# adaLN steps in groups of three from three buffers, none until the RWKV scan is over; pairs in the FFN

## The chip, the cores and the metric

The kernel runs on one core of one Trainium2 chip. The metric is the device time of the execution in microseconds (us); the time before is the median of three runs. TensorE (PE in the profile) multiplies matrices, VectorE (DVE), ScalarE (ACT) and GpSimd (POOL) do the elementwise work, and SyncE (SP) issues nearly all DMA transfers, in the order of its queue.

## The reference, cut to what matters

One layer of a diffusion backbone, in float32, with D = 2048, 256 latent tokens and 256 context tokens. The parts that the change touches are the adaLN vectors and what uses them:

```python
mod_x = (jax.nn.silu(c) @ w_mod[l] + b_mod[l])[:, None, :]          # w_mod: 2048 x 12288
sh1x, sc1x, gt1x, sh2x, sc2x, gt2x = jnp.split(mod_x, 6, axis=-1)
ux = modulate(rms_norm(x, norm_g[l, 0]), sh1x, sc1x)
mc, mx = token_mixers(uc, ux, p, not last)                            # conv, mLSTM, GDN, RWKV, gates, merge, w_out
x = x + gt1x * rms_norm(mx, norm_g[l, 1])
fx = conv_ffn(modulate(rms_norm(x, norm_g[l, 2]), sh2x, sc2x), ffn_up[l], ffn_dw[l], ffn_down[l], True)
x = x + gt2x * rms_norm(fx, norm_g[l, 3])
```

`token_mixers` projects the modulated input with w_in into the columns of four branches and four sets of gates, runs three chunked scans in two directions (RWKV, gated DeltaNet or GDN, mLSTM) and a convolution module, multiplies each branch by its w_br, sums them under sigmoid gates and multiplies by w_out.

## The kernel before, in words

**Column sets.** A weight matrix is read in loads of 256 x 512 floats (512 KB, `raw`). ScalarE rounds each to `hi` (fp32r) and VectorE subtracts to get `lo` (lines 198 and 200); the activations are kept split the same way (`uh`, `ul`). A set of 512 columns takes eight loads ("kg"). `mode_b` makes columns by tokens (`psB`), `mode_a` tokens by columns (`psA`); each kg costs three products per 128 rows, per block or token tile, all issued in `mm` (line 79). After each kg both call `feed()`.

**adaLN steps.** `wmod_steps` makes 512 columns of the adaLN vector in eight steps: each loads 512 KB of w_mod (`wraw`, line 260) and issues four products of 32 columns (`psw`; the profile has eight records a step). The eighth is followed by a copy of the sums (`wrows`), products that spread them (`psf`) and an addition of the bias into `mod2`, or, for the two gain vectors `G[0]` and `G[1]`, an addition and a product by the norm's gain over 128 partitions, with two 256 KB rows loaded into `wbg`. `psw` and `psf` take turns in the one PSUM bank of the pool `wap` before the FFN, and in the two banks of `auxf` in it. The opening stage makes the first eight blocks itself, from a pool of seven buffers. `mod_feed` is the generator of the rest: eight blocks of `mod2` (64 steps), four of G[0] (32), four of G[1] (32). `feed()` adds `rate` to `fed` and takes steps until `modn` has caught up, up to `modmax`.

**Order.** `build` calls, one after another: the opening stage, RWKV columns and scan, GDN columns, mLSTM columns, conv columns, two gate column sets, the RWKV output, the GDN scan, the conv module, the mLSTM scan, the sixteen column sets of `gates` (16 x 8 kgs), four `merge`s (16 column sets of two kgs each, so 32 kgs), `out_proj` (w_out), and `ffn`. The program is ordered by a scheduler that follows these priorities and a timing model, so scans are threaded through the column sets that come after them in the source: the scans' small products run as they become ready, and column products fill the time between. The order on each engine and in the SP queue is then fixed. Gates write their sigmoids to HBM (`dg`); a merge reads them back (`sig`) and accumulates in `mg`.

**The pace before.** `rate` is 0 until the mLSTM columns, 0.55 from there, 0 again after the gates; in the FFN it is 0.25, after a first block of eight steps at its start (`feed(96 + 8)`). Step loads go into the pool `wmr` with one buffer; in the FFN they take a tile of the ring of `raw` (five).

**SBUF.** Pools are placed when the scheduler reaches them, where there is room; a tile in a reused place waits until the tiles that were there have been read. `g1p` holds G[0] and is opened in `gd_scan`; `mqT` and `mkT` lie in the mLSTM scan's pool `mrp`; `mgw` (for `sig`), `mgp` (for `mg`) and `hlp` (a second ring of hi and lo for the last set of `out_proj`) are opened after the gates, in this order. `stage` hands out tiles of 512 floats from `fs` under the tags f0 to f3.

Of the kernel before, what the change touches and what calls it, by code (L numbers as in the profile page):

```python
# [11 lines left out]
F32 = mybir.dt.float32  # L12
# [8 lines left out]
P = 128  # L21
D = 2048
# [19 lines left out]
class Kern:  # L42
# [205 lines left out]
    def wmod_steps(self, cb, dst, raws=None, gain=None):  # L248


        nc, A = self.nc, self.A
        if raws is not None and cb in (0, 4):
            ps = self.mmp.tile([P, 512], F32, tag="mm", name="psw")
        else:
            ps = (self.evp if self.wap is not None else self.aux)("psw")
        w = A["w_mod"][0]
        for j in range(8):
            wr = raws or self.wmr
            raw = self.raw() if wr is None else wr.tile([P, 2, 512], F32, tag="wraw", name="wraw")
            nc.sync.dma_start(out=raw, in_=w[256 * j : 256 * j + 256, 512 * cb : 512 * cb + 512].rearrange("(k p) c -> p k c", p=P))  # L260
            for k in range(2):
                for h in range(2):
                    r = slice(64 * h + 32 * k, 64 * h + 32 * k + 32)
                    self.mm(ps[r, 0:256], self.cst[:, 2 * j + k, :], raw[:, k, 256 * h : 256 * h + 256], start=(j == 0), stop=(j == 7))
            if j < 7:
                yield
        rows = self.stage("f3", 256, "wrows")
        nc.scalar.activation(rows, ps[:, 0:256], AF.Copy)
        if gain is not None:

            bg = self.stage("f2", 512, "wbg"), self.stage("f2", 512, "wbg")
            for t, row in zip(bg, (A["b_mod"][0], gain)):
                c0 = 512 * cb if row is not gain else 512 * (cb % 4)
                nc.sync.dma_start(out=t, in_=row[c0 : c0 + 512].unsqueeze(0).to_broadcast([P, 512]))
            ps = (self.evp if self.wap is not None else self.aux)("psf")
            for h in range(2):
                self.mm(ps[:, 256 * h : 256 * h + 256], self.selb[:, h], rows)
            nc.vector.tensor_tensor(dst, ps, bg[0], ALU.add)
            nc.gpsimd.tensor_tensor(dst, dst, bg[1], ALU.mult)
            yield  # L280
            return
        ps = (self.evp if self.wap is not None and raws is None else self.aux)("psf")
        for i in range(2):
            self.mm(ps[:, 4 * i : 4 * i + 4], rows[:, P * i : P * i + P], self.sel4.rearrange("p h c -> p (h c)"))
        n = dst.shape[2]
        bm = self.PC["b_mod"][:, 4 * cb : 4 * cb + 4].unsqueeze(2).to_broadcast([P, 4, n])
        for h in range(2):
            nc.vector.tensor_tensor(dst[:, 2 * h : 2 * h + 2], ps[:, 0:8].rearrange("p (i h c) -> p h i c", h=2, c=2)[:, h, :, 0:n],
                                    bm[:, 2 * h : 2 * h + 2], ALU.add)
        yield  # L290
# [14 lines left out]
    def feed(self, upto=0):  # L305

        self.fed += self.rate
        while self.modn < max(upto, min(self.fed, self.modmax)):
            self.modn += 1
            next(self.modgen)  # L310

# [183 lines left out]

    def stage(self, tag, shape, name):

        t = self.fs.tile([P, 512], F32, tag=tag, name=name)
        return t if shape == 512 else t[:, 0:shape]

    def rw_k_steps(self):
# [517 lines left out]
    def gd_scan(self):  # L1019
# [2 lines left out]
        ges = ExitStack()  # L1022
        up = self.pool("gup", stack=ges, side="right")
        wp = self.pool("gwp", bufs=2, stack=ges, side="right")
        self.G[0] = self.pool("g1p", stack=self.ues).tile([P, D], F32, name="G1")
        tp = self.pool("gtp", stack=ges, side="right")
        lg, beta = self.lg, self.beta
        b4 = lambda ap, r=P: ap.unsqueeze(2).to_broadcast([r, 4, P])
# [22 lines left out]
        for nm, src in (("negc", negc), ("egc", egc), ("erem", erem), ("beta", beta)):  # L1051
            t = m4[nm] = gp.tile([P, 2, 4, 4], F32, name="gm" + nm)
# [18 lines left out]
        for seg in range(2):  # L1071
# [5 lines left out]
            for jj in range(2):  # L1077
# [13 lines left out]
                for h in range(4):  # L1091
                    for c in range(2):
                        r = slice(64 * c, 64 * c + 64)
                        t = slice(P * jj + 64 * c, P * jj + 64 * c + 64)
# [10 lines left out]
            for i in range(4):  # L1105
# [6 lines left out]
                for d in range(2):  # L1112
                    t = slice(256 * seg + 64 * ch[d], 256 * seg + 64 * ch[d] + 64)
# [69 lines left out]
    def ml_scan(self):  # L1183
        nc = self.nc
        self.mlx = ExitStack()
        mp = self.pool("mrp", stack=self.mlx)
        wa = self.pool("mwa", bufs=2, stack=self.mlx)
        wp = self.pool("mwb", bufs=2, stack=self.mlx)
        mqT, mkT = mp.tile([P, 4, 256], F32, name="mqT"), mp.tile([P, 4, 512], F32, name="mkT")
        mv = mp.tile([P, 4, 4, 132], F32, name="mv")  # L1190
        nc.gpsimd.memset(mv[:, :, :, 128:129], 1.0)
        nc.sync.dma_start(out=mqT, in_=self.dmq)
# [231 lines left out]
    def ffn(self):  # L1424
        nc, A, PC = self.nc, self.A, self.PC
        x = self.x1
        ues = ExitStack()
# [9 lines left out]
            nc.vector.tensor_scalar(diag[:, i], self.ident, rs[i], None, ALU.mult)  # L1437
        sc = fp.tile([P, KT], F32, name="sc2")
        nc.vector.scalar_tensor_tensor(sc, self.mod2[:, 16:32, 0], 1.0, PC["ng"][:, 32:48], ALU.add, ALU.mult)
        self.fs = self.pool("ffs", bufs=2)  # L1440
        self.wap, self.rate, self.modmax = None, 0.25, 128
        self.G[1] = fp.tile([P, D], F32, name="G2")
        self.feed(96 + 8)
# [101 lines left out]
    def build(self):  # L1545
        tc = self.tc
        pes = ExitStack()
        self.auxs = None
        self.aux_pool("auxp", aux=3)
        self.wap = self.pool("wap", bufs=1, space=PSUM, stack=pes)  # L1550
        self.mmp = self.pool("mmp", bufs=4, space=PSUM, stack=pes)
        self.constants()
        self.dp = self.pool("dp", space=bass.MemoryType.DRAM)
        ses = ExitStack()
        self.rawp = self.pool("rawp", bufs=4, stack=ses)
        self.hip = self.pool("hip", bufs=2, stack=ses)
        self.lop = self.pool("lop", bufs=2, stack=ses)
        ues = self.ues = ExitStack()
        self.up = self.pool("up", stack=ues)
        bp = self.bp = self.pool("bp", stack=ues)  # L1560
        self.wmr = self.pool("wmr", bufs=1, stack=ues)
        self.xes = ExitStack()
        self.x2 = self.pool("x2", stack=self.xes)
        fes = ExitStack()
        self.fs = self.pool("fs", bufs=2, stack=fes, side="right")
        res = ExitStack()
        rq = self.rqp = self.pool("rqp", stack=res, side="right")
        T = lambda nm, s: rq.tile(s, F32, name=nm)
        self.sxg = T("sxg", [P, 2, 256])
        self.bv = T("bv", [P, 4, 256])  # L1570
        self.res = res
        self.rwx = ExitStack()
        self.fed, self.rate, self.modn, self.modmax = 0.0, 0.0, 0, 96
        self.pool_lo = 0
        self.mod2, self.G = self.cp.tile([P, 32, 1], F32, name="mod2"), [None, None]
        self.modgen = self.mod_feed()
        self.phase0(self.rw_k_steps, self.rw_open)
        self.aux_pool("auxp2", aux=3)
        self.rw_columns()
        self.token_gates(bp)  # L1580
        self.rw_feat()
        self.aux_pool("auxr", u=2, s=1)
        self.rw_scan()
        self.gd_columns()
        self.rate = 0.55
        self.ml_columns()
        self.conv_columns()
        self.gz = self.gate_columns(C_GDZ, AF.Silu, "gz")
        self.mo = self.gate_columns(C_MLO, AF.Sigmoid, "mo")
        self.rw_out()  # L1590
        self.aux_pool("auxg", aux=3)
        res.close()
        ces = ExitStack()
        self.gop = self.pool("gop", stack=ces, side="right")
        self.cvp = self.pool("cvp", stack=ces, side="right")
        self.gd_scan()
        self.gd_out()
        self.conv_module()
        ces.close()
        self.ml_scan()  # L1600
        self.gates()
        self.feed(96)
        self.rate = 0.0
        fes.close()
        self.dbg("yh", self.uh[:, :, 0:256].bitcast(F32))
        self.dbg("yl", self.ul[:, :, 0:256].bitcast(F32))
        self.mgw = self.pool("mgw", bufs=3, stack=ues)
        self.mgp = self.pool("mgp", stack=ues)
        self.mg = self.mgp.tile([P, 2, D], F32, name="mg")
        self.hlp = self.pool("hlp", bufs=2, stack=ues)  # L1610
        self.resp = self.pool("resp", side="right")
        self.x1 = self.resp.tile([P, 2, D], F32, name="x1")
        self.ffdw = self.resp.tile([P, 396], F32, name="ffdw")
        self.nc.sync.dma_start(out=self.ffdw, in_=self.A["taps"])
        for i, n in enumerate((3, 0, 2, 1)):
            self.merge(i == 0, n)
        self.out_proj()
        self.wmr = None
        ues.close()
        ses.close()  # L1620
        pes.close()
        self.aux_pool("auxf", aux=2)
        self.es.callback(self.auxs.close)
        mes = ExitStack()
        self.mmp = self.pool("mmp2", bufs=6, space=PSUM, stack=mes)
        self.rawp = self.pool("rawp2", bufs=5)
        self.hip = self.pool("hip2", bufs=4)
        self.lop = self.pool("lop2", bufs=4)
        self.mmes = mes
        self.ffn()  # L1630

# [54 lines left out]
```

## Time and profile before

| | |
|---|---|
| median of 3 runs | 2329.59 us (2325.4 to 2334.24) |
| the profiled execution | 2329.05 us, span 2327.1 us, mean granted TensorE clock 0.977 |
| TensorE busy | 2215.9 us (95%) |
| VectorE, ScalarE, GpSimd busy | 1449.6, 989.5, 507.6 us |
| DMA | 471.97 MB, mean 203 GB/s |
| w_mod loads from wraw / raw | 160 / 32 of 512 KB |

The span is from the first to the last instruction; what lies around it is 1.9 us. TensorE's busy time counts products that overlap one another, and products that wait inside the array, so the cadence of starts in the timeline says more of its speed than the busy share. Rows of a timeline give start, duration, engine, line, operation, out<-in, tile and count, and in brackets the idle time before and what ended it. Rows of waits give the total, the number and the longest, in us.

### The profile page before, as it was taken

Reading aid. Unit: us, or ns where it says so; the run is one execution under the profiler, and the core shown is the slowest. Engines: PE = TensorE matmul, PEld = TensorE weight load, DVE = VectorE, ACT = ScalarE, POOL = GpSimd, SP = SyncE. Lnnn points to the kernel's source line nnn. Section 1 sums busy time; section 2 is a strip of 40 time slices with the busy share of each in tenths; the row PEclk is TensorE's granted clock in tenths of the full one; section 3 lists DMA queues with packets and bytes.
Section 4 is the critical chain, followed back from the end, with each engine's and each line's share of the span. In section 5 each row is a group of like instructions: output and inputs, shape, how many; then the busy total and the mean of one; then the engine's idle time right before and its main releaser. Section 6 shows DMA issues by size and latency. Waiting matters only on the chain.

```text
span 2327.1 us, 42867 instructions
## 1 busy us (share of the span) xinstructions
PE 2215.9 (95%) x16828; PEld 1812.0 (78%) x16828; DVE 1449.6 (62%) x3027; ACT 989.5 (43%) x1493; POOL 507.6 (22%) x865
## 2 busy tenths in 40 slices
PE   6979889999999989999999899989999999999998
PEld 3657667877888666777777678779999999998886
DVE  3357766734555678457565476577776677775554
ACT  4225644533554344334236434444443444444443
POOL 0012553533454599210010033010000000000000
PEclk8989999999999999999999999989999999999999
DMA  9934663555666776787777476567677666666663
GB/s 369 352 115 127 170 183 113 159 171 170 199 188 180 231 208 209 231 247 237 226 231 256 139 257 217 181 231 222 212 222 217 202 182 183 179 205 202 194 193 101
DMA packets 273867, 471.97 MB, mean 203 GB/s; under 512 B 41761, under 2 KB 80929, under 8 KB 272673
## 3 DMA queue, kind: packets, MB, share of 16 engines
q1 hardware_dynamic: 273378, 467.14, 64.8%
q8 instruction: 132, 2.16, 0.4%
q10 hardware_dynamic: 288, 2.10, 0.2%
q14 instruction: 69, 0.57, 0.1%
HBM read 440.33 MB, written 28.84 MB: 202 GB/s over the span
## 4 chain that ended last, share of the span: by engine, by line
PE 78%; DVE 8%; DMA 7%; POOL 4%; ACT 2%; issue 2%; SPq 0%; DVEq 0%; ACTq 0%; POOLq 0%
PE psB L79 37%; PE psA L79 18%; PE psD L79 10%; PE psw L79 4%; DMA wraw<-in_w_mod 3%; DVE lo L200 2%; POOL ctap L874 1%; DMA raw<-in_w_mix 1%; PE psG L79 1%; POOL cacc L875 1%; ACT hi L198 1%; PE psn L79 1%; DMA raw<-in_w_in 1%; PE psf L79 1%; DVE cacc L869 1%
## 5 line engine op out<-in xcount | busy, mean ns | idle before, releaser
L200 DVE TENSOR_TENSOR lo<-raw,hi 128x1024 fp32r<-128x1024 f32 (+2 forms) x485 | 599.2, 1236 | 458.7 <-ACT hi L198 450.0
L198 ACT ACTIVATE hi<-raw 128x1024 fp32r<-128x1024 f32 (+2 forms) x488 | 509.2, 1045 | 796.5 <-PE psB L79 348.6
L79 PE MATMUL psB<-u2h,hi 128*128 128x256 f32 x1408 | 399.5, 286 | 1.2 <-DVE u2h L1370 1.2
L79 PE MATMUL psB<-u2l,hi 128*128 128x256 f32 x1408 | 398.8, 284 | 0.5 <-DVE u2l L1371 0.5
L79 PE MATMUL psB<-u2h,lo 128*128 128x256 f32 x1408 | 399.0, 284 | 0.0
L79 PE MATMUL psA<-lo,uh 128*128 128x512 f32 x832 | 337.4, 406 | 18.4 <-DVE lo L200 18.0
L79 PE MATMUL psA<-hi,ul 128*128 128x512 f32 x832 | 332.7, 400 | 0.0
L79 PE MATMUL psA<-hi,uh 128*128 128x512 f32 x832 | 311.4, 405 | 3.2 <-DVE mg L1344 2.1
L79 PE MATMUL psB<-uh,hi 128*128 128x256 f32 (+1 forms) x832 | 281.0, 346 | 18.7 <-ACT hi L198 16.4
L79 PE MATMUL psB<-ul,hi 128*128 128x256 f32 (+2 forms) x832 | 278.5, 339 | 0.0
L79 PEld LDWEIGHTS psB<-u2h,hi 128*128 128x128 f32 x1408 | 269.6, 192 | 10.9 <-issue 9.5
L79 PEld LDWEIGHTS psB<-u2l,hi 128*128 128x128 f32 x1408 | 270.5, 192 | 0.7 <-DVE u2l L1371 0.7
L79 PE MATMUL psB<-uh,lo 128*128 128x256 f32 (+2 forms) x832 | 263.0, 339 | 8.1 <-DVE lo L200 8.1
L79 PEld LDWEIGHTS psB<-u2h,lo 128*128 128x128 f32 x1408 | 270.5, 192 | 0.1
L79 PEld LDWEIGHTS psA<-lo,uh 128*128 128x128 f32 x832 | 158.1, 190 | 68.5 <-DVE lo L200 27.5
L79 PEld LDWEIGHTS psB<-uh,hi 128*128 128x128 f32 x832 | 158.6, 191 | 51.2 <-ACT hi L198 18.5
L79 PEld LDWEIGHTS psA<-hi,uh 128*128 128x128 f32 x832 | 154.7, 190 | 53.2 <-issue 12.2
L79 PEld LDWEIGHTS psA<-hi,ul 128*128 128x128 f32 x832 | 158.3, 190 | 36.5 <-issue 2.6
L79 PEld LDWEIGHTS psB<-uh,lo 128*128 128x128 f32 (+1 forms) x832 | 152.8, 189 | 32.0 <-DVE lo L200 10.5
L79 PEld LDWEIGHTS psB<-ul,hi 128*128 128x128 f32 (+1 forms) x832 | 157.8, 190 | 23.1 <-issue 6.4
L1541 DVE TENSOR_TENSOR lo<-raw,hi 128x1024 fp32r<-128x1024 f32 x88 | 107.7, 1226 | 78.5 <-ACT hi L1540 78.5
L1461 DVE SCALAR_TENSOR_TENSOR facc<-fpad,ffdw,facc 128x256 f32<-128x256 f32 x352 | 152.8, 490 | 0.2
(573 smaller groups left out, 3028.8 us busy)
## 6 DMA issues: line engine op xcount, KB each, us to landing
raw<-in_w_in SPq DMA_DIRECT2D x208, 512.0 KB, 4.3
raw<-in_ffn_up SPq DMA_DIRECT2D x176, 512.0 KB, 3.8
wraw<-in_w_mod SPq DMA_DIRECT2D x160, 512.0 KB, 5.1
raw<-in_ffn_down SPq DMA_DIRECT2D x88, 512.0 KB, 4.5
raw<-in_w_br SPq DMA_DIRECT2D x32, 512.0 KB, 5.1
raw<-in_w_out SPq DMA_DIRECT2D x32, 512.0 KB, 4.4
raw<-in_w_mod SPq DMA_DIRECT2D x32, 512.0 KB, 3.8
raw<-in_w_in SPq DMA_DIRECT2D x48, 256.0 KB, 4.1
```

Source lines behind the costliest of these rows:

```text
L79: self.nc.tensor.matmul(out, lhsT, rhs, start=start, stop=stop)
L198: nc.scalar.activation(hi[s], raw[s], AF.Copy)
L200: (nc.gpsimd if self.pool_lo >= 0 else nc.vector).tensor_tensor(lo[s], raw[s], hi[s].bitcast(F32), ALU.subtract)
L869: nc.vector.scalar_tensor_tensor(a, cpad[:, i, t : t + 256], w(i, t), a, ALU.mult, ALU.add)
L874: nc.gpsimd.tensor_scalar(m, cpad[:, i, t : t + 256], w(i, t), None, ALU.mult)
L875: nc.gpsimd.tensor_tensor(a, a, m, ALU.add)
L1461: nc.vector.scalar_tensor_tensor(s3(acc), pad[:, dy : dy + 4, dx : dx + 64], tap(t, b), s3(acc), ALU.mult, ALU.add)
L1541: nc.vector.tensor_tensor(f(lo), f(raw), f(hi).bitcast(F32), ALU.subtract)
```

## The change

Steps are taken in groups: `feed` rounds what is due down to a multiple of `group`, 3 up to the merges and 2 in the FFN. `rate` stays 0 through all column sets and scans in the source and becomes 0.6 before `gates`; it goes on through the merges, after which `feed(96)` takes what is left. `wmr` has three buffers and is opened after the RWKV output; in the FFN a new `wmr2` has two, and steps no longer use `raw`. G[0] gets its place after the mLSTM scan. `mqT` and `mkT` get a pool of their own; `mg` is placed ahead of `mgw`; staging in the merges comes from a new pool `fsm`, which is closed with `mgw` before `hlp` is opened. In the FFN the staging tag f3 is 256 floats wide instead of 512. No product, load or elementwise operation is added or removed.

```diff
@@ wmod_steps
-            raw = self.raw() if wr is None else wr.tile([P, 2, 512], F32, tag="wraw", name="wraw")
+            raw = wr.tile([P, 2, 512], F32, tag="wraw", name="wraw")
@@ feed
         self.fed += self.rate
-        while self.modn < max(upto, min(self.fed, self.modmax)):
+        due = int(min(self.fed, self.modmax)) // self.group * self.group
+        while self.modn < max(upto, due):
@@ stage
-        t = self.fs.tile([P, 512], F32, tag=tag, name=name)
+        t = self.fs.tile([P, self.fw.get(tag, 512)], F32, tag=tag, name=name)
@@ gd_scan
-        self.G[0] = self.pool("g1p", stack=self.ues).tile([P, D], F32, name="G1")
@@ ml_scan
-        mqT, mkT = mp.tile([P, 4, 256], F32, name="mqT"), mp.tile([P, 4, 512], F32, name="mkT")
+        qk = self.pool("mqk", stack=self.mlx)
+        mqT, mkT = qk.tile([P, 4, 256], F32, name="mqT"), qk.tile([P, 4, 512], F32, name="mkT")
@@ ffn
-        self.fs = self.pool("ffs", bufs=2)
+        self.fs, self.fw = self.pool("ffs", bufs=2), {"f3": 256}
@@ build
-        self.wmr = self.pool("wmr", bufs=1, stack=ues)
...
-        self.fed, self.rate, self.modn, self.modmax = 0.0, 0.0, 0, 96
+        self.fed, self.rate, self.modn, self.modmax, self.group = 0.0, 0.0, 0, 96, 3
...
         self.gd_columns()
-        self.rate = 0.55
         self.ml_columns()
...
         ces = ExitStack()
+        self.wmr = self.pool("wmr", bufs=3, stack=ues)
...
         self.ml_scan()
+        self.G[0] = self.pool("g1p", stack=ues).tile([P, D], F32, name="G1")
+        self.rate = 0.6
         self.gates()
-        self.feed(96)
-        self.rate = 0.0
         fes.close()
-        self.mgw = self.pool("mgw", bufs=3, stack=ues)
         self.mgp = self.pool("mgp", stack=ues)
         self.mg = self.mgp.tile([P, 2, D], F32, name="mg")
-        self.hlp = self.pool("hlp", bufs=2, stack=ues)
+        mes = ExitStack()
+        self.fs = self.pool("fsm", bufs=2, stack=mes)
+        self.mgw = self.pool("mgw", bufs=3, stack=mes)
...
             self.merge(i == 0, n)
+        self.feed(96)
+        self.rate = 0.0
+        mes.close()
+        self.hlp = self.pool("hlp", bufs=2, stack=ues)
         self.out_proj()
-        self.wmr = None
...
+        self.wmr, self.group = self.pool("wmr2", bufs=2), 2
         self.mmes = mes
         self.ffn()
```

More of the change, by code (lines that the diff above doesn't have):

```diff
@@ L1564, in build @@
         fes = ExitStack()
-        self.fs = self.pool("fs", bufs=2, stack=fes, side="right")
+        self.fs, self.fw = self.pool("fs", bufs=2, stack=fes, side="right"), {}
         res = ExitStack()
```

## The prediction

> **What bounds the kernel now.** I read the page's engine table and chain first.
>
> ```profile
> span 2327.1 us, 42867 instructions
> ...
> PE 2215.9 (95%) x16828; PEld 1812.0 (78%) x16828; DVE 1449.6 (62%) x3027; ACT 989.5 (43%) x1493; POOL 507.6 (22%) x865
> ...
> PE 78%; DVE 8%; DMA 7%; POOL 4%; ACT 2%; issue 2%; SPq 0%; DVEq 0%; ACTq 0%; POOLq 0%
> PE psB L79 37%; PE psA L79 18%; PE psD L79 10%; PE psw L79 4%; DMA wraw<-in_w_mod 3%; DVE lo L200 2%; POOL ctap L874 1%; DMA raw<-in_w_mix 1%; PE psG L79 1%; POOL cacc L875 1%; ACT hi L198 1%; PE psn L79 1%; DMA raw<-in_w_in 1%; PE psf L79 1%; DVE cacc L869 1%
> ```
>
> TensorE is busy 95% of the span and carries 78% of the chain; the adaLN products (psw) are 4% of it and the wait for their weights 3%. That is an average, so next come the windows by stage (us; PE, PEld, DVE, ACT, POOL busy; clock; DMA share; GB/s): the column sets beside the RWKV scan (470 to 756), gates beside the conv module and the GDN scan (to 1280), the mLSTM scan's end (1280 to 1372; its worst part is 1303 to 1342), the merges (1342 to 1427), and a stretch of the start as the measure of a full DMA.
>
> ```profile
> 470.00:756.00 286.00, 286.00 (x3423) 231.19 (x3422) 141.44 (x542) 124.28 (x248) 119.28 (x349) 1.00 0.61 181
> 756.00:935.00 179.00, 162.78 (x1171) 115.59 (x1171) 138.83 (x281) 71.05 (x98) 144.09 (x145) 0.97 0.72 215
> 935.00:1280.00 345.00, 340.42 (x2671) 248.60 (x2666) 199.75 (x438) 138.80 (x184) 36.56 (x39) 1.00 0.78 239
> 1303.00:1342.00 39.00, 29.74 (x134) 23.12 (x132) 14.78 (x36) 12.56 (x29) 0.70 (x1) 0.82 0.36 123
> 1342.00:1427.00 85.00, 83.17 (x360) 66.33 (x361) 63.29 (x87) 32.01 (x38) 38.42 (x24) 0.98 0.79 269
> 58.20:116.40 58.20, 57.46 (x431) 37.24 (x423) 19.37 (x42) 13.88 (x21) 0.00 (x0) 1.00 1.00 352
> ```
>
> From 470 to 756 TensorE has no idle time at all, so an instruction taken from it there is time, unless a scan beside it sets the pace. From 935 to 1280 4.6 us are idle; at 1303 to 1342 nine are, at a clock of 0.82.
>
> **Price of a step, alone and in a row.** The timeline of TensorE around one step in the gates (eight records), then around five steps in a row in the opening stage:
>
> ```profile
> 1063.65 0.39 PE L79 MATMUL psA<-lo,uh 128*128 128x512 f32 x1
> 1063.88 0.39 PE L79 MATMUL psA<-hi,ul 128*128 128x512 f32 x1
> 1064.20 0.64 PE L79 MATMUL psw<-wraw,cst 128*32 128x256 f32 x8
> 1064.77 0.73 PE L79 MATMUL psA<-hi,uh 128*128 128x512 f32 x2
> 1065.34 0.39 PE L79 MATMUL psA<-lo,uh 128*128 128x512 f32 x1
> ...
> 63.87 2.37 PE L79 MATMUL psw<-wraw,cst 128*32 128x256 f32 x40
> 66.17 0.50 PE L79 MATMUL psB<-uh,hi 128*128 128x512 f32 x1
> ```
>
> Column products start 0.23 us apart. Around the lone step, three such starts (1063.88 to 1065.34) take 1.46 instead of 0.69: it costs 0.77 us. Five in a row take 2.30 from first start to the next psB; less the 0.57 from a lone step's start to its successor, four more cost 1.73, or 0.43 each. So a step directly behind another saves 0.34 us. Which steps are alone now is in the windows of the psw rows alone (PE and PEld busy, then ACT where the group has any):
>
> ```profile
> 470.00:756.00 286.00, 22.20 (x232) 5.35 (x232) 1.00 0.61 181
> 756.00:1300.00 544.00, 44.01 (x528) 10.78 (x528) 0.99 0.75 227
> 1570.00:2060.00 490.00, 14.06 (x176) 3.46 (x176) 1.10 (x3) 1.00 0.67 203
> ```
>
> 29 steps among the columns (0.77 us each), 66 from 756 on (0.67) and 22 in the FFN (0.64), nearly all lone; one more lies before 470.
>
> **The change part by part.** *Pace.* A feed comes after each of the kg loops. Before: 56 of them in the mLSTM, conv and gate columns at 0.55 give 31 steps, the rest come in the gates' 128. After: none in the columns; 0.6 over 128 feeds of gates and 32 of merges makes 96, in threes every fifth feed, 77 by the end of the gates and 19 in the merges. So the columns lose 31 steps (23.9 us at 0.77), the gates go from 65 to 77 steps, and the merges get 19, 10.3 us of TensorE at 0.77 + 2 x 0.43 = 1.63 per three.
>
> *Groups of three.* 32 groups, two steps of each behind another: 64 x 0.34 = 21.8 us less if all stay whole. A block has 8 steps, so 8 of the 12 blocks end inside a group; there the one PSUM bank (wap) must pass through ACT, psf and DVE before the next step, and other products go between. With some groups cut by a scan's products I keep 80%: **-17.4**. Ends: 0 and -21.8.
>
> *Three buffers.* Waits of TensorE from 935 to 1280, and of SP's queue from 756 to 1300:
>
> ```profile
> PE psw L79 <- DMA wraw<-in_w_mod: 4.0, 8, 1.2
> PE psA L79 <- DVE lo L200: 0.4, 1, 0.4
> ...
> SPq L194 <- DVE lo L200: 197.4, 78, 5.3
> SPq L260 <- PE psw L79: 53.5, 45, 3.1
> ```
>
> With one buffer a load is issued only behind the last step's products; SP then stands 53.5 us with the raw loads queued behind it, and TensorE waits 4.0. With three freed five feeds earlier both go: **-4.0** (ends 0 and -4.0); SP next waits for raw slots, as it does now for 197.4. Each moved step takes its load through the same SP queue, now three together, 1.57 MB, 4.5 us at 352 GB/s ahead of the next raw load; the four raw tiles cover 4 x 12 x 0.23 = 11 us. I cost it nothing; without that cover it is up to 4.5 us a group.
>
> *Places in SBUF* (wmr, mqk, G1, mgw behind mg, fsm, hlp): no instruction, but other waits on reused places. The timeline at the mLSTM scan's end:
>
> ```profile
> 1312.67 1.73 PE L79 MATMUL psn<-mv,mA 128*128 128x129 f32 x14
> ...
> 1336.81 3.35 PE L79 MATMUL psn<-mv,mA 128*128 128x129 f32 x14 [1.79 <-ACT mA L1259]
> ...
> 1342.25 0.50 PE L79 MATMUL psA<-hi,uh 128*128 128x512 f32 x1 [2.09 <-DVE mg L1344]
> ...
> 1341.51 2.48 DVE L1344 TENSOR_TENSOR mg<-sig,psA 128x512 f32<-128x512 f32 x4
> ```
>
> The merges fill their four PSUM banks and stop until mg is first written, after the scan's last psn. With other places that write can come up to 25 us earlier (1317, where the fill ended) or some 15 later, and the gates and columns run dry sooner, since 23.9 + 9 us of TensorE work leave ahead of this point. As TensorE never waits for a scan from 470 to 1280, I let the scans move up with it and take **+3** for a longer hole (ends -10 and +33). hlp's first use is three column sets of out_proj later (66 us); f3 at 256 and the dropped fallback to raw cost nothing.
>
> *Merges.* 85 us x 269 GB/s = 22.9 MB now; 19 loads of 512 KB and three pairs of 256 KB rows (wbg; sizes in the next fence) add 11.5 MB. 34.4 MB at 352 GB/s is 98 us, against 85 + 10.3 of TensorE: **+3** (ends 0 and +13). The Trainium skill ("DMA: Bandwidth & Descriptors", Measured) has 425 GB/s for a 16 MB transfer; by it the merges would take 81 us of DMA, this term would be 0 and the sum 3 us lower. No row quoted here is above 352.
>
> *FFN.* Pairs: of 22 lone steps 11 come to stand behind another, 11 x 0.34 = **-3.7** (ends 0, -3.7). But the first block of eight now has two buffers where it had five raw tiles:
>
> ```profile
> 1505.67 7.87 SPq L260 DMA_DIRECT2D raw<-in_w_mod  x5
> ...
> 1519.87 2.37 PE L79 MATMUL psw<-raw,cst 128*32 128x256 f32 x40
> ...
> 1534.48 2.67 PE L79 MATMUL psts<-ffdiag,x 128*128 128x128 f32 x10 [1.78 <-DVE ffdiag L1437]
> ...
> wraw<-in_w_mod SPq DMA_DIRECT2D x160, 512.0 KB, 5.1
> ...
> raw<-in_w_mod SPq DMA_DIRECT2D x32, 512.0 KB, 3.8
> ...
> wbg<-in_b_mod SPq DMA_DIRECT2D x8, 256.0 KB, 3.7
> ```
>
> Five loads are issued before out_proj ends and run as one row at 1519.87; the transposes wait for ffdiag until 1534.48. With two buffers it takes four rounds of 3.8 + 0.6 = 17.6 us, and if the place is out_proj's until 1519.5 the block ends at 1537 and holds one of two PSUM banks for 3 us of the transposes: **+2** (ends -1, +8). The five raw tiles then belong to ffn_up.
>
> **Sum**: -17.4 - 4.0 + 3 + 3 - 3.7 + 2 = -17.1. The profiled execution took 2329.05 us (span 2327.1 and 1.9 around it), the median of the three runs is 2329.59: 2329.05 - 17.1 = **2312**.
>
> **Rivals.** *The groups fall apart.* The loads of a group land one after another, and the order within TensorE's queue is made from ready times; if the steps are put singly into gaps, only the waits (-4.0) go and +8 of the costs stay, with nothing from the pairs: 2333 at worst, 2329 with half of those costs. For it: eight block ends inside groups. Against: all three loads can be issued five feeds ahead. *The scans set the pace (slower).* For: TensorE waits for ACT and DVE of the mLSTM scan from 1317 on. Against: no such wait before. Then nothing that leaves ahead of 1342 is gained, the hole grows, and the merges carry their 19 steps at the pace of the DMA: +13, FFN -3.7 + 2, and two more sets of psn at the low clock (3.35 against 1.73 us) +3.2: 2329 + 14.5 = 2343.5. It decides once more than about 20 of the 32.9 us come back as idle TensorE. The Trainium skill ("TensorE: Matmul & The Clock Gate", Part 1) halves the clock after about 3.4 us idle; the 0.82 above with waits of 2 us fits a partly cold stretch, and a longer hole would be colder. *The hole is filled.* Steps and merges run while the scan ends because mg comes early: -10 instead of +3, 2299. For: loads need only a free buffer. Against: G1's blocks need psf's bank.
>
> **Numbers.** Forecast 0.50 (own range 2301 to 2321), groups apart 0.22, scans 0.16, hole filled 0.12. A measurement of this kernel tells about 0.5% from no change, 2317.9 and 2341.2 here. Faster: the third and all below 2317.9 of the first, 0.12 + 0.40 = 0.52; slower: most of the scans' case, 0.13; same 0.35. Range 2298 to 2337: the filled hole to the groups apart, and the lower part of the scans' case.
>
> **What would show it.** psw rows of x24 (x16 in the FFN), none from 470 to 760, and TensorE's busy psw time per step near 0.5; no wait of psw for wraw; the gates' start earlier by some 20 us; DMA in the merges near 340 GB/s. Wrong would make it: psw rows of x8, idle of TensorE between the gates' end and mg's first write longer than 40 us, psA waiting for raw loads behind three wraw loads, or psts waiting past 1540 relative to out_proj's end.

## The result, and the profile after

The changed kernel takes 2354.11 us (median of 4 runs, 2351.78 to 2359.92) against 2327.49 for the kernel before: a ratio of 1.012, 95% interval 1.0105 to 1.0135. It is slower by 26.6 us, where 2312 was forecast. The profiled execution took 2354.46 us. From its page, the span, the engines and the group of adaLN products (busy, mean ns of one | idle before them and its releaser):

```profile
span 2352.5 us, 42883 instructions
...
PE 2219.5 (94%) x16828; PEld 1810.3 (77%) x16828; DVE 1450.7 (62%) x3027; ACT 980.9 (42%) x1488; POOL 505.9 (22%) x865
...
L79 PE MATMUL psw<-wraw,cst 128*32 128x256 f32 x1536 | 130.3, 407 | 47.6 <-DMA wraw<-in_w_mod 43.8
```

TensorE is busy 3.6 us longer than before, though groups were to save it time. psw waits 43.8 us for its own loads: 20.2 of them up to 470 us (22.2 before), 0.6 from 756 to 1300, and 23.0 at the start of the FFN, where steps waited 3.5 before. Three windows of the prediction, then the psw rows alone by stage:

```profile
470.00:756.00 286.00, 283.75 (x3275) 242.76 (x3274) 149.96 (x543) 137.03 (x262) 115.71 (x333) 1.00 0.50 145
...
1303.00:1342.00 39.00, 25.02 (x104) 17.72 (x105) 13.59 (x42) 5.63 (x19) 3.34 (x3) 0.63 0.30 91
1342.00:1427.00 85.00, 84.70 (x436) 61.64 (x434) 58.22 (x66) 29.95 (x35) 36.02 (x23) 1.00 0.92 332
```
```profile
470.00:756.00 286.00, 0.00 (x0) 0.00 (x0) 0.00 (x0) 1.00 0.50 145
756.00:1300.00 544.00, 57.77 (x640) 17.82 (x640) 3.36 (x9) 0.99 0.76 238
1300.00:1427.00 127.00, 11.91 (x128) 3.50 (x128) 1.11 (x3) 0.87 0.71 250
1570.00:2060.00 490.00, 13.46 (x192) 5.12 (x192) 1.15 (x3) 1.00 0.67 200
```

No step is left from 470 to 756, 80 stand from 756 to 1300 and 16 behind it. A step in the gates is busy for 57.77 / 80 = 0.72 us; before it was 0.67. At 1303 to 1342 TensorE is 14 us idle (9 before) at a clock of 0.63 (0.82 before). The timeline says how this stretch ends (TensorE, then VectorE, then the SP queue):

```profile
1324.65 3.35 PE L79 MATMUL psn<-mv,mA 128*128 128x129 f32 x14 [1.79 <-ACT mA L1260]
...
1333.19 2.79 PE L79 MATMUL psw<-wraw,cst 128*32 128x256 f32 x24 [3.52 <-DVE G L278]
1337.55 0.79 PE L79 MATMUL psA<-hi,uh 128*128 128x512 f32 x1 [1.56 <-DVE mg L1345]
...
1336.80 1.28 DVE L1345 TENSOR_TENSOR mg<-sig,psA 128x512 f32<-128x512 f32 x2 [3.66 <-DMA sig<-dg]
...
1328.15 0.34 SPq L274 DMA_DIRECT2D wbg<-in_b_mod  x1
...
1329.35 2.02 SPq L1339 DMA_DIRECT2D sig<-dg  x3
```

The gates' sigmoids on ScalarE and the scan's psn products, by first and last start (the view by tile), before and then after the change:

```profile
L1326 ACT ACTIVATE sig<-psA x32: 584/598/602, 800.1 to 1300.1; 128x512 f32<-128x512 f32 x32
L79 PE MATMUL psn<-mv,mA x112: 271/275/554, 1259.5 to 1339.7; 128*128 128x129 f32 x112
```
```profile
L1327 ACT ACTIVATE sig<-psA x32: 592/597/600, 754.2 to 1271.8; 128x512 f32<-128x512 f32 x32
L79 PE MATMUL psn<-mv,mA x112: 271/275/554, 1257.6 to 1327.6; 128*128 128x129 f32 x112
```

The gates end 28.3 us earlier (1271.8 against 1300.1), but the scan starts only 1.9 us earlier. Its last row of psn comes 12.2 us earlier (1324.65 against 1336.81), mg's first write only 4.7 (1336.80 against 1341.51): the gates' lead is mostly gone in the scan's exposed tail (its last part, beside which TensorE has no other work), and part of the rest while sig is loaded. Of the scan's 112 psn products 46 had started when the last gate was done before the change, and 18 after it. The waits of SP's queue from 1270 to 1450 name what held sig's loads:

```profile
SPq L274 <- PE psn L79: 36.4, 1, 36.4
```

One wbg load waits 36.4 us for the last psn, because the merges' staging lies where the scan's mA lies; sig stands behind it in the queue. (The first tile of sig also lies over the scan's last dn, so two places hold it.) Next the start of the FFN (TensorE, then SP):

```profile
1527.52 0.40 PE L79 MATMUL psA<-hi,ul 128*128 128x512 f32 x1
1531.61 0.64 PE L79 MATMUL psw<-wraw,cst 128*32 128x256 f32 x8 [3.70 <-DMA wraw<-in_w_mod]
...
1561.23 2.96 PE L79 MATMUL psts<-ffdiag,x 128*128 128x128 f32 x12
...
1527.71 0.88 SPq L260 DMA_DIRECT2D wraw<-in_w_mod  x2
1528.64 2.23 SPq L194 DMA_DIRECT2D raw<-in_ffn_up  x4
```

Before, five loads were issued from 1505.67 on, ahead of out_proj's end, and the first five steps ran as one row. Now the first load is issued at 1527.71, behind out_proj's last product: the two buffers lie over uh, which out_proj's products read to the end. The long row of transposes comes 33.7 us behind that product (1561.23 against 1527.52); before it came 14.9 us behind it (1534.48 against 1519.54). Last, ffn_down, ten starts of psD apart, after the change and then before it:

```profile
2149.75 0.39 PE L79 MATMUL psD<-hi,hh 128*128 128x512 f32 x1
...
2152.09 0.39 PE L79 MATMUL psD<-lo,hh 128*128 128x512 f32 x1
```
```profile
2149.79 0.39 PE L79 MATMUL psD<-lo,hh 128*128 128x512 f32 x1
...
2152.06 0.39 PE L79 MATMUL psD<-hi,hl 128*128 128x512 f32 x1
```

That is 0.234 us a product against 0.227, with the same instructions. Their first and last starts (the view by tile; durations min/median/max in ns ahead of them), before and after:

```profile
L79 PE MATMUL psD<-hi,hh x352: 389/389/632, 2075.5 to 2316.8; 128*128 128x512 f32 x176
```
```profile
L79 PE MATMUL psD<-hi,hh x352: 392/392/500, 2095.4 to 2342.3; 128*128 128x512 f32 x176
```

So the 25.4 us between the two spans are: mg's first write -4.7; from it to out_proj's last product (1519.54 before) +12.7; from there to the first psD +11.9; psD +5.6 (246.9 against 241.3).

### The profile page after: what moved, and what is told of

Its sections match the earlier page's. It is cut to its first block, busy times and chain, and to the rows that moved or that the text cites. A ratio compares the mean times of both kernels' runs of the same rounds, so it can differ in the third digit from the quotient of the medians.

```text
span 2352.5 us, 42883 instructions
## 1 busy us (share of the span) xinstructions
PE 2219.5 (94%) x16828; PEld 1810.3 (77%) x16828; DVE 1450.7 (62%) x3027; ACT 980.9 (42%) x1488; POOL 505.9 (22%) x865
## 4 chain that ended last, share of the span: by engine, by line
PE 79%; DVE 9%; DMA 4%; ACT 3%; POOL 3%; issue 2%; SPq 0%; DVEq 0%; POOLq 0%; ACTq 0%
PE psB L79 35%; PE psA L79 20%; PE psD L79 10%; PE psw L79 4%; DVE lo L200 2%; DMA raw<-in_w_mix 1%; DMA wraw<-in_w_mod 1%; DVE cacc L870 1%; POOL riU L404 1%; ACT hi L198 1%; PE psG L79 1%; POOL rim L403 1%; PE psn L79 1%; PE psf L79 1%; PE psr L79 0%
## 5 line engine op out<-in xcount | busy, mean ns | idle before, releaser
L79 PEld LDWEIGHTS psA<-hi,uh 128*128 128x128 f32 x832 | 154.1, 190 | 50.2 <-issue 12.2
L79 PEld LDWEIGHTS psB<-uh,lo 128*128 128x128 f32 (+1 forms) x832 | 150.7, 189 | 32.4 <-DVE lo L200 12.2
L79 PE MATMUL psw<-wraw,cst 128*32 128x256 f32 x1536 | 130.3, 407 | 47.6 <-DMA wraw<-in_w_mod 43.8
```

Source lines behind the costliest of these rows:

```text
L79: self.nc.tensor.matmul(out, lhsT, rhs, start=start, stop=stop)
```

## The experiments

Each kernel ran beside the kernel before on the same chip. The four series gave 2326.75 (first four kernels), 2328.48 (next four), 2327.66 (next three) and 2328.59 us (the last) for that one, where the changed kernel's own series had 2327.49; so a difference to the changed kernel's 2354.11 is uncertain by about 1 us beyond the scatter of the runs.

### 1. First block from the raw tiles

```diff
+        keep, self.wmr = self.wmr, None      # self.raw() in wmod_steps
         self.feed(96 + 8)
+        self.wmr = keep
```

> The changed kernel, with the first block of eight steps in the FFN loaded into the five raw tiles again; the pairs after it keep their two buffers, and every pool keeps its place. Theory 'two buffers': in the changed trace the first psB of the FFN follows the last product of out_proj by 36 us, before by 20; the eight loads through two buffers, with ffn_up's raw loads between them in the SP queue, cost the difference of 15 us. Then the psw products of the first block run as one row right after out_proj again, and the time is 2354 - 15 = 2339 (2336 to 2343). Rival 'late diagonal': the FFN starts late because the residual and ffdiag are late, whatever the loads do; then the steps only wait elsewhere and the time stays at 2350 to 2355. psD keeps its cadence of 233 ns in both, since nothing moves in SBUF.

Measured 2345.11 us, ratio 1.007 (1.0048 to 1.0092): 9.0 less than the changed kernel, not 15. The SP queue shows the rest:

```profile
1528.85 0.88 SPq L260 DMA_DIRECT2D wraw<-in_w_mod  x2
1529.77 9.80 SPq L260 DMA_DIRECT2D raw<-in_w_mod  x8
```

The pairs' first two loads stand ahead of the eight raw loads and wait for uh. The loss has two parts, rounds through two buffers and a place that is free too late; only the first was undone, and the transposes still come 20.3 us behind out_proj's last product.

### 2. The FFN of the kernel before

```diff
-        self.wmr, self.group = self.pool("wmr2", bufs=2), 2
+        self.wmr, self.group = None, 1        # and f3 512 wide
```

> The changed kernel up to the end of out_proj, and the FFN of the kernel before (single steps from the raw tiles, f3 of 512, no buffers of its own). Theory 'places': the products psD ran every 226.7 ns before and every 233.3 ns after, 1056 times, with the same instructions, because hi, lo, hh and hl lie in other places; here hh lies at a third place (152512 of each partition; 172992 before, 216160 after), so the cadence need be neither. With 227 ns: 2354 - 15 (first block) + 3 (no pairs) - 5.5 = 2336.5; with 233 ns: 2342. Rival 'clock': psD was slower because that execution's clock or its DMA were; then the cadence comes out by chance and will not hold between kernels of one layout. What remains against before (2327.5) is then the first half: 2336.5 - 2327.5 = +9 by the first theory.

Measured 2340.18 us, 1.0053 (1.0037 to 1.0068): 13.9 less than the changed kernel. psD's cadence is back at 0.227 us, with hh at a third place. With psD at 5.6 and the lost pairs at some -2, the first block was worth some 10 of it.

### 3. All steps in the gates

```diff
-        self.rate = 0.6
+        self.rate = 0.75
```

> The changed kernel with the pace 0.75 in place of 0.6 in the gates: all 96 steps are due by the end of the gates and none are left for the merges. Theory 'scans set the pace' (the GDN and mLSTM scans stood at the same times within 6 us in both traces while the column sets ran 20 to 50 us earlier, so TensorE's work beside them is free until mg's first write): 21 steps leave the merges, which cost 10.7 us there, mg's first write stays within 3 us of where it is, and the time is 2354 - 10 = 2344 (2341 to 2347). Rival 'every step costs its products wherever it stands' (the prediction's): 2352 to 2355, with mg's first write 9 to 11 us later. Rival 'DMA': 96 loads beside the gates hold up raw loads, psA waits, 2356 or more.

Measured 2386.56 us, 1.0247 (1.0228 to 1.0266), far above the first two ranges. It lies in the third (2356 or more), but not for the reason given there: psA's waits for lo did not grow (12.8 us from 756 to 1300, 15.9 in the changed kernel's two windows). A part comes from my edit: the pace went on counting, so 24 steps instead of 8 became due at the start of the FFN. TensorE's waits from 1500 to 1620 and the first write of mg:

```profile
PE psw L79 <- DMA wraw<-in_w_mod: 44.5, 21, 6.5
```
```profile
L1345 DVE TENSOR_TENSOR mg<-sig,psA x8: 676/680/686, 1346.9 to 1362.3; 128x512 f32<-128x512 f32 x8
```

The part that the edit did not spoil: mg's first write came 10.1 us later (1346.9 against 1336.8), close to the 11.9 us that the 16 steps behind 1300 had been busy. Steps in the gates are not free.

### 4. Without 32 steps in the columns

```diff
-        for i in range(8):
+        for i in range(4, 8):                 # mod2 blocks; pace from the gates on
```

> The kernel before without the 32 steps that it takes in the mLSTM, conv and gate columns (the first four blocks of mod2 are left out, with their loads, products and additions; everything from the gates on keeps its steps). The prediction's term: those columns are TensorE-bound, so 32 steps at 0.77 us leave the time: 2327.5 - 24.6 = 2303. Theory 'scans set the pace': the gates end some 25 us earlier, the idle stretch at the mLSTM scan's end grows by about as much, mg's first write moves by 0 to 6 us, and the time is 2321 to 2327.

Measured 2326.04 us, 0.9993 (0.9981 to 1.0005): nothing, where the prediction's term had 24.6. The window of the scan's end, then the scan's psn (duration min/median/max, first and last start) and mg:

```profile
1303.00:1342.00 39.00, 26.45 (x106) 21.35 (x106) 10.41 (x33) 8.24 (x29) 0.00 (x0) 0.68 0.00 0
```
```profile
L79 PE MATMUL psn<-mv,mA x112: 272/422/555, 1279.0 to 1341.0; 128*128 128x129 f32 x112
```
```profile
L1344 DVE TENSOR_TENSOR mg<-sig,psA x8: 677/679/687, 1342.8 to 1357.4; 128x512 f32<-128x512 f32 x8
```

The gates were done some 30 us earlier, but the mLSTM scan began later (1279.0 against 1259.5 before) and ended where it had ended; none of its psn products had started when the last gate was done, where 46 had before. TensorE waited for it, at a clock of 0.68, with no DMA at all. The scheduler moves later steps up, so in time 18 of the 32 are missing from 470 to 756 and 13 behind 756.

### 5. Without 32 steps in the gates

```diff
-        for k, row in ((0, 1), (1, 3)):
+        for k, row in ((1, 3),):              # G[0] left out, modmax 64
```

> The kernel before without 32 of its steps in the gates (G[0]'s four blocks are left out, with loads, products and gain; the steps stop half way through the gates). The counterpart of leaving out 32 steps in the columns, which moved the time from 2326.75 to 2326.04 only. Theory 'the scans' place in the order sets mg's first write': 2322 to 2328, mg's first write within 6 us of 1341.5, and the idle stretch at the mLSTM scan's end grows. Rival 'only the columns are free': the mLSTM scan's own products are threaded between gate products, so each step less there lets the scan advance; 32 x 0.67 = 21 us less, 2305, with mg's first write near 1320. In the changed kernel with 96 steps in the gates that write came 10.6 us later than with 75, which speaks for the rival.

Measured 2316.73 us, 0.9943 (0.9926 to 0.996), 11.8 us less: between the two theories.

```profile
L1345 DVE TENSOR_TENSOR mg<-sig,psA x8: 679/680/689, 1330.5 to 1346.3; 128x512 f32<-128x512 f32 x8
```

mg is written 11.0 us earlier, half of what the products take. The 32 steps are all missing from 950 us on, in the late gates. There they were worth half their price, in run 4 nothing. The order differs too: here the scan starts at 1253.4, earlier than before (1259.5), in run 4 at 1279.0. So the two runs don't separate where a step stands from when the scheduler starts the scan.

### 6. Other places for sig, mg and the staging

```diff
+        self.mgw = self.pool("mgw", bufs=3, stack=ues)
         self.mgp = self.pool("mgp", stack=ues)
...
-        self.mgw = self.pool("mgw", bufs=3, stack=mes)
```

> The changed kernel with other places: the pool of sig (mgw) is opened ahead of mg and lies over the staging of the gates, mg over the mLSTM scan's mA, the merges' staging (fsm) over mqT and mkT; the second ring of hi and lo becomes two pools of half the size. Theory 'place': in the changed trace SP's queue stood 36 us at a wbg load whose place lies under mA, until the last psn at 1327.6, with sig's loads behind it, and mg was first written at 1336.8, 9 us after that psn (1.8 us before the change). Here sig and wbg can be loaded during the scan, mg's first write comes 2 us after the last psn, and the time is 2354 - 7 = 2347 (2345 to 2349). Rival 'the merges are full anyway': the 21 steps and 34 MB of loads in the merges set their end, the earlier start only lengthens them, and the time stays at 2351 to 2356.

Measured 2344.14 us, 1.0061 (1.0042 to 1.008): 10.0 less than the changed kernel. TensorE in the scan's tail:

```profile
1316.47 1.50 PE L79 MATMUL psw<-wraw,cst 128*32 128x256 f32 x24 [2.26 <-DVE G L278]
1317.90 1.83 PE L79 MATMUL psn<-mv,mA 128*128 128x129 f32 x14
...
1326.97 3.38 PE L79 MATMUL psn<-mv,mA 128*128 128x129 f32 x14
1330.28 1.71 PE L79 MATMUL psw<-wraw,cst 128*32 128x256 f32 x16
```

mg is written at 1331.70, 5.1 us earlier, and steps that stood in the merges now run between the scan's products, where TensorE waited. The second effect was not expected and is at least as large as the first: from mg's first write to out_proj's last product the trace has 8.9 us less.

### 7. hh and hl moved in the kernel before

```diff
+        pad = self.pool("ffpad").tile([P, 2900], F32, name="ffpad")     # and f3 256 wide
         wp = self.pool("ffw", bufs=2)
```

> The kernel before with hh and hl of ffn_down moved in SBUF: an unused tile of 11.6 KB is placed behind ffp so that their pool lands at 217632 of each partition instead of 170944 (f3 is 256 wide in the FFN, as after the change); nothing else changes. Theory 'place': psD's cadence goes from 226.7 ns to about 233 ns, as in the changed kernel (hh at 216160) and unlike the kernel with hh at 152512 (226.7 ns): 1056 x 6.6 ns = +7, 2334. Rival 'neighbour': hi and lo of ffn_down, which also lie elsewhere after the change, set it; here they stay, so the cadence stays 226.7 ns and the time 2326.5.

Measured 2337.55 us, 1.0037 (1.0026 to 1.0047). Ten starts take 2.34 us instead of 2.27:

```profile
2149.79 0.39 PE L79 MATMUL psD<-lo,hh 128*128 128x512 f32 x1
...
2152.13 0.39 PE L79 MATMUL psD<-hi,hl 128*128 128x512 f32 x1
```

Of what psD reads, only hh and hl lie elsewhere than in the kernel before; hi and lo stay. So the place of hh and hl does it: 1056 x 7 ns = 7.4 of the 9.1 us.

### 8. All 128 steps ahead of the merges

```diff
-        self.rate = 0.55
+        self.rate = 1.1        # columns; gates 0.55, modmax 128; G[1] through HBM
```

> A version meant to be faster than both: the kernel before with all 128 steps ahead of the merges. The pace in the mLSTM, conv and gate columns is doubled to 1.1 (62 steps there instead of 31), the gates keep 0.55 and take the rest, so G[1]'s 32 steps leave the FFN; each of its four blocks is stored as a row and read back in the FFN. No step runs in the FFN. Theory 'columns free' (32 steps less in the columns changed the time by -0.7 us, the scan's end by 1): 32 more cost 0 to 8 us there, because the idle stretch at the scan's end takes them up; the FFN loses 22 steps of 0.64 us and the two last beside its end, 14 to 16 us: 2311 to 2320. Rival 'every step costs its products': 31 x 0.77 = 24 us more ahead of mg, 15 less in the FFN: 2335.

Measured 2369.46 us, 1.017 (1.0155 to 1.0185), worse than the rival's 2335. TensorE's waits from 1350 to 1610:

```profile
PE psw L79 <- DMA wraw<-in_w_mod: 18.8, 6, 8.0
PE psts L79 <- issue: 18.6, 1, 18.6
```

mg's first write came at 1404.2. One buffer did not carry the pace, and the last steps ran singly behind the scan, each waiting for its load. Why the transposes waited 18.6 us at the FFN's start, where the first block had been, the profile doesn't name. Removing steps from the columns changes nothing, but it does not follow that adding them does.

### 9. Groups of one

```diff
-        ... self.modmax, self.group = 0.0, 0.0, 0, 96, 3
+        ... self.modmax, self.group = 0.0, 0.0, 0, 96, 1
```

> The changed kernel with groups of one ahead of the FFN: the pace, the three buffers and all places stay, each step becomes due alone. The prediction's term: 64 of 96 steps stand behind another and save 0.34 us each, 80% of it kept; without the groups +17, 2371. Theory 'the groups fell apart': in the changed trace the 96 steps ahead of out_proj stand as 85 uninterrupted pieces of psw products (before: 95 as 104), because other products are put between; the most that groups of one can cost is the rest of the pieces, 11 x 0.33 = 4, and the time is 2350 to 2358.

Measured 2356.47 us, 1.0128 (1.0108 to 1.0148): 2.4 above the changed kernel, within its scatter, not 17. TensorE's timelines in the gates, of the changed kernel and then of groups of one:

```profile
962.55 1.05 PE L79 MATMUL psw<-wraw,cst 128*32 128x256 f32 x10
963.53 1.09 PE L79 MATMUL pVN<-gX,gU 64*64 64x128 f32 x16
...
967.99 0.63 PE L79 MATMUL psw<-wraw,cst 128*32 128x256 f32 x6
```
```profile
965.40 1.05 PE L79 MATMUL psw<-wraw,cst 128*32 128x256 f32 x10
966.38 1.09 PE L79 MATMUL pVN<-gX,gU 64*64 64x128 f32 x16
...
970.84 0.63 PE L79 MATMUL psw<-wraw,cst 128*32 128x256 f32 x6
```

The scan's pVN cuts into the second step, and the rest of it follows 4.5 us later. With groups of one the same rows stand 2.85 us later: the order on TensorE is nearly the same in both, and the 96 steps ahead of out_proj stand as 85 uninterrupted pieces in either trace (105 before the change). So this run doesn't price whole groups against single steps. It shows that `group` hardly reached the order of the engine.

### 10. The places and the FFN together

The edits of 2 and 6.

> The changed kernel with two of its costs undone together: sig, mg and the merges' staging in the places that gave 2344 instead of 2354, and the FFN of the kernel before, which alone gave 2340. What remains of the change is the pace (no step in the columns, 80 in the gates, 16 behind them), groups of three and three buffers. Theory 'additive': 2354 - 10 - 14 = 2330 (2327 to 2334), so that the pace and the groups by themselves are worth nothing against the kernel before (2327 to 2328.5). Rival 'overlap': both undo the same delay in the SP queue ahead of the FFN, and the time stays at 2337 to 2341. Second rival, the prediction's first terms: pace and groups gain 15 to 20 by themselves, 2310.

Measured 2332.48 us, 1.0018 (1.0006 to 1.003), 4.8 above the kernel before: additive within 2.5 us. What the pace and the groups win up to the end of out_proj doesn't last. TensorE at the FFN's start:

```profile
1514.83 0.40 PE L79 MATMUL psA<-hi,ul 128*128 128x512 f32 x1
1523.73 1.08 PE L79 MATMUL psw<-raw,cst 128*32 128x256 f32 x8 [8.51 <-DMA raw<-in_w_mod]
```

out_proj ends at 1514.83, 4.7 us earlier than before (1519.54), and then TensorE waits 8.5 us for loads into raw tiles that now lie over G[0], which out_proj reads to its end.

### 11. Steps behind the gates

```diff
+        self.rate = 0.55       # columns, single, raw tiles; gates 0.35 in threes
...
         self.gates()
+        self.feed(96)          # the last 20, ahead of the merges
```

> A version meant to beat both: the places of the run before it in this list and the FFN of the kernel before; 31 single steps in the column sets at 0.55 (their loads take raw tiles), then three buffers and groups of three at 0.35 in the gates (45 steps, 65 before the change), and the last 20 steps at once behind the gates, ahead of the merges in the program, where TensorE waits for the mLSTM scan. From the runs: 32 steps taken out of the columns gave -0.7 us, 32 taken out of the late gates -11.8, so 20 steps fewer there give about -7; the 20 behind the gates fill waits at 0 to +5. 2320 to 2327. Rival 'order': the scan advances only as its products are placed, the 20 steps delay its end, and the time is 2328 to 2334.

Measured 2325.85 us, 0.9993 (0.9982 to 1.0004): as before. out_proj ends 7.3 us earlier (its last product starts at 1512.28) and then TensorE waits 8.2 us for the FFN's first load, much as in 10.

### 12. The same, with the raw tiles in their old place

```diff
+        gap = self.pool("gap", stack=ues).tile([P, 1536], F32, name="gap")
         self.out_proj()
```

> The version with early steps behind the gates (2325.85) and one unused tile of 6 KB opened ahead of out_proj, so that the FFN's five raw tiles lie where the old raw tiles were and not over G[0], as in the kernel before. In the trace of the version without it out_proj's products run 7.2 us earlier than before (1493.8 against 1501.0 at the same product), but the first load of the FFN's steps stands in the SP queue behind a wbg load until 1512.7, and TensorE waits 8.2 us for it; by the first psD nothing is left of the 7. Theory 'place': here five of these loads are issued before out_proj ends, the FFN starts 20 us behind out_proj's last product as before, and the time is 2326 - 7 = 2319 (2316 to 2322), faster than both kernels. Rival 'late diagonal': the transposes of the FFN wait for ffdiag, which takes as long behind out_proj whatever the loads do; then the time stays at 2324 to 2327.

Measured 2323.48 us, 0.9974 (0.9959 to 0.9989): faster than the kernel before by 0.26%, short of the 2319 expected. An unused tile of 6 KB moves the raw tiles:

```profile
1513.72 2.37 PE L79 MATMUL psw<-raw,cst 128*32 128x256 f32 x40
```

The first five steps are one row again, right behind out_proj. It is the fastest kernel of the study that leaves nothing out, by a margin smaller than what was called measurable for one kernel alone.

## Why the prediction was wrong, by its own steps

- *Pace and places*, +3: the step that cost most is "I let the scans move up with it". The prediction let 32.9 us of TensorE work leave ahead of mg's first write and set 3 against them, so steps taken out of the columns were worth their full price. The gates did end 28.3 us earlier, but the scan started 1.9 us earlier and mg's first write came 4.7 us earlier. The lead ended in the scan's tail, as the second rival had it: 32 steps fewer in the columns gave 0.7 us (run 4). The size of the places' term was wrong too: run 6 puts it at 10.
- *Price of a step*: this held as a duration: a lone row of eight records takes 0.64 us before and after.
- *Groups of three*, -17.4: this term failed. I let block ends and the scans' products take 20%; but the scan's products cut groups, even steps, anywhere, and busy time per step in the gates rose from 0.67 to 0.72, where it was to fall. That the steps come apart is the first rival's case. What it lacked is that groups of one run in nearly the same order, 2.4 us slower (run 9).
- *Three buffers*, -4.0: TensorE's wait went as said (935 to 1280: before 4.0 us for wraw in 8 waits; now only psA <- lo, 1.9, is listed), but SP's did not: it stands 76.1 us behind psw from 756 to 1300, where it stood 53.5. Pace, groups and buffers together won 4.7 us up to out_proj's end once the places were right (run 10).

```profile
SPq L260 <- PE psw L79: 76.1, 48, 3.6
```

- *Merges*: their steps, 10.3, were counted as moved, and +3 for DMA. From mg to the end of out_proj 12.7 us were added, with 332 GB/s in the merges: right in size. The transfer share was 0.92, so the DMA limit that I took from the opening stage was near, not passed; nor is 352 GB/s a ceiling, since the first slice of the page before has 369. The count was off: in threes 76.8 due steps round down to 75, so the program left 21 to the merges and not 19, and in time 80 stood ahead of 1300.
- *FFN pairs*, -3.7: busy psw went from 14.06 us for 22 steps to 13.46 for 24, from 0.64 to 0.56 a step or 1.9 us in all; the sign was right, the term about twice that.
- *FFN first block*, +2 (ends -1 and +8): 10 (run 2) to 14 (the 11.9 of the trace and the pairs' 2). I took the place to be free when out_proj ends, and left out that the loads can then not be issued ahead, and that ffn_up's raw loads stand between them in the queue.
- *psD* stood in no term: 5.6 us from where hh and hl lie.

The second rival (2343.5) had the tail and the merges' 13; it let the scan's end lose 3 us where 4.7 were won, and lacked the larger first block and psD. What stays open is why the scan did not move up with the gates, and began 20 us later in run 4: the profile shows the order on TensorE, not what the scheduler weighed.

## What to carry to other kernels

Before crediting a saving in a stage where TensorE is always busy, look whether the same order has an idle stretch further on that waits for a chain threaded through that stage; the saving lands there first. A run with the work simply left out tells, if you also look whether the order of the rest has changed. A pool that is added or reordered moves every later one, so look what each new place lies over and which instruction reads that last: in this kernel the places of staging, buffers and raw tiles moved 2 to 10 us each (runs 12 and 6) through a queue that serves in order. Before pricing a group that the program makes, see in a trace whether the group reaches the engine: here a scheduler stood between, and threes and ones ran in nearly the same order.

## What the runs showed of the hardware

The cadence of psD's 128x512 products depends on where their stationary operand (hh or hl) lies in the partition. Their starts are 0.227 us apart with hh at byte 152512 and 172992 of the partition, 0.234 at 216160 and 219680, with the same instructions. The Trainium skill ("TensorE: Matmul & The Clock Gate", section "Wait — 56ns, not 53.3ns?") gives 215.7 ns for 512 columns at the full clock; no two starts of psD are that close in the two traces (226 ns at least), and the section doesn't speak of places. Which property of the place counts, these four values can't tell.

The scan's tail pays twice, in waits and in slower products. Before the change fourteen psn products take 1.73 us between column products (the row at 1312.67, granted clock 1.00) and 3.35 where TensorE waits between them (the row at 1336.81, granted clock 0.50); the last row after the change also takes 3.35 at 0.50. By the Trainium skill's same page, Part 1, the clock is halved after an idle window of about 3.4 us. The clock in these rows agrees with the halving; the wait shown ahead of the last psn is 1.79 us, shorter than that window, and the rows don't tell which waits halved it.
